# The gate products of a bidirectional RG-LRU as pairs of 64-row tiles, with the gates brought together by transfers on chip

## The chip, the core and the metric

The kernel runs on one core of one Trainium2 chip. The metric is device microseconds (us) of one execution; the number for a kernel is the median of its runs. TensorE (PE) does the matrix products into PSUM banks, ScalarE (ACT) does casts, activations and most evictions of banks, VectorE (DVE) does element-wise work and the recurrence scans, and the DMA queue that SyncE (SP) issues brings the weights in. Each engine works through its own instructions in the order in which they stand in the program and waits in that order.

## What is computed

Two layers of a diffusion backbone over 768 tokens (256 of context, 512 latent) of width 1024. Each layer mixes tokens by four branches (retention, latent attention, RG-LRU, Mamba-2), merges them by gates, and runs a gated feed-forward network. The change touches the RG-LRU alone:

```python
def gates(u, d):
    ub = u.reshape(b, t, LRU_BLOCKS, LRU_BLOCK)          # 8 blocks of 64 channels
    z = jnp.einsum('btnc,gncd->gbtnd', ub, gate_w[d])    # g: two gates, r and i
    z = z.reshape(2, b, t, w) + gate_b[d]
    r, i = jax.nn.sigmoid(z[0]), jax.nn.sigmoid(z[1])
    log_a = -LRU_C * r * jax.nn.softplus(-lam[d])
    return jnp.exp(log_a), jnp.sqrt(-jnp.expm1(2.0 * log_a)) * (i * u)
# run(u, d): a, bb = gates(u, d); h = linear scan h[t] = a[t] * h[t-1] + bb[t]
# both directions d, context first, and the latent tokens from its last state
```

## The kernel before, in words

Channels lie on the 128 partitions and tokens along the free axis. Every product is done as three float32r matmuls (`mm3`, L219 to L222): operands are split into a rounded high part and a low part, and high·high, high·low and low·high are summed in one PSUM bank. A weight of 512 KB is loaded by SP (L198, tile wr), its high part is cast by ACT (L205, tile wh), and its low part is a subtraction on DVE (L143, tile wl).

The 512 channels of the recurrence are four groups f of 128, and each group holds two of the 64-channel blocks. `project(f)` makes the convolved input u and the gelu gate (two products with eight row blocks each; evictions L511 and L1045 on ACT, the convolution on DVE at L152). `scan(f, d)` is called for both directions d, so there are 4 groups x 2 directions x 2 layers = 16 scans. A scan

- splits u (direction 0 alone) by the cast at L216 on ACT and the subtraction at L143 on DVE;
- forms both gates z as products with a 128x128 weight in which the two 64x64 blocks stand on the diagonal and the rest is zero, for a segment of 256 and one of 512 tokens: 4 banks (pool `c`, four banks in all), 12 matmuls;
- evicts each bank by a Tanh on ACT (L1066) into t0 (gate r) or t1 (gate i), 128 partitions each;
- forms the decay on ACT by an Exp (L1069) and a Tanh (L1070) of t0 and a Sqrt (L1074, which has a table load ahead of it), and on DVE the products with t1 and the scan itself (L1079 to L1082).

The bias column of each gate is in the small tile gb, half the stored bias (L549 to L551). The gate weights of two groups come as one 128x1024 load (L1056).

The order of instructions is set ahead of time by a planner that weaves the recurrence into the `merge` of an earlier branch: long runs of PE products (L220 to L222 into banks of pool `g`, also four) are put between the steps of a scan, and the merge's evictions (Tanh, L1334, on ACT) stand among the scan's activations. In layer 0, runs of small products at L317 for the modulation are put in as well (in tiles of 128 rows by 32 columns). The recurrence of layer 0 lies at about 765 to 950 us of the span, that of layer 1 at about 2240 to 2380 us.

Of the kernel before, what the change touches and what calls it, by code (L numbers as in the profile page):

```python
# [8 lines left out]
F32 = mybir.dt.float32  # L9
F32R = mybir.dt.float32r  # L10
AF = mybir.ActivationFunctionType
# [20 lines left out]
SEG_C = (0, CTX)  # L32
# [66 lines left out]
def trunk(tc, xin, cc, const, pv, pr, rows, ada_b, ada_w, w_in, w_uq, w_ukv, w_lg, w_br, w_out, w_up, w_dn, out):  # L99
# [3 lines left out]
    def nm(p):  # L103
        uid[0] += 1
        return f"{p}{uid[0]}"
# [3 lines left out]
    with ExitStack() as ctx:  # L109
# [14 lines left out]
        def S(dt=F32, w=T):  # L124
            return cur[-1].tile([P, w], dt, tag="q" if w == 512 and len(cur) == 2 else "s", name=nm("s"), **({"bufs": N_HALF} if w == 512 and len(cur) == 2 else {}))
# [4 lines left out]
        def C():  # L130
            return pc.tile([P, 512], F32, tag="c", name=nm("c"))
# [13 lines left out]
        def ts(o, a, s1, op0, s2=None, op1=None):  # L145
            if s2 is None:
                dve.tensor_scalar(out=o, in0=a, scalar1=s1, scalar2=None, op0=op0)
            else:
                dve.tensor_scalar(out=o, in0=a, scalar1=s1, scalar2=s2, op0=op0, op1=op1)
# [51 lines left out]
        def unit(ap, f=1024, shape=None):  # L201
            with tc.high_priority(offset=O_UNIT):
                raw = whole(ap, f)
                hi = W4("wh", N_WH)
                act.copy(hi[:, 0:f], raw[:, 0:f])  # L205
                lo = W4("wl", N_WL)
                for c in range(0, f, 512):
                    e = min(f, c + 512)
                    tt(lo[:, c:e], raw[:, c:e], hi[:, c:e].bitcast(F32), SUB)
            if shape is None:  # L210
                return hi, lo
            a, b = shape
            return (hi[:, 0:f].rearrange("p (a b) -> p a b", a=a), lo[:, 0:f].rearrange("p (a b) -> p a b", a=a))

        def split(src, hi, lo):
            act.copy(hi, src)  # L216
            tt(lo, src, hi.bitcast(F32), SUB)
# [302 lines left out]
        def layer_prep(l):  # L520
            q = {}
            v = lp.tile([P, NPV], F32, tag="pv", name=nm("pv"))
            sy.dma_start(out=v, in_=pv[l])
            r = lp.tile([P, NPR], F32, tag="pr", name=nm("pr"))
            sy.dma_start(out=r, in_=pr[l:l + 1, :].to_broadcast([P, NPR]))

            def V(name, a=0, b=None):
                o, w = _PO[name]
                return v[:, o + a:o + (w if b is None else b)]

            q["V"] = V

            z = small(16, "z")
            dve.tensor_copy(z[:, 0:8], r[:, 0:8])
            dve.tensor_copy(z[:, 8:16], V("lam"))
            u = small(16, "z")
            exp_negabs(u, z, 16)
            lgp = small(16, "z")
            log1p_of(lgp, u, 16)
            lg = lp.tile([P, 8], F32, tag="lgr", name=nm("lgr"))  # L540
            stt(lg, z[:, 0:8], 0.0, lgp[:, 0:8], MIN, SUB)
            spv = small(16, "z")
            ts(spv[:, 0:8], z[:, 8:16], -1.0, MUL, 0.0, MAX)
            tt(spv[:, 0:8], spv[:, 0:8], lgp[:, 8:16], ADD)
            l4 = lp.tile([P, 16], F32, tag="l4", name=nm("l4"))
            ts(l4[:, 0:8], spv[:, 0:8], -4.0, MUL)
            ts(l4[:, 8:16], spv[:, 0:8], 4.0, MUL)
            q["l4"] = l4
            gb = lp.tile([P, 16], F32, tag="gb", name=nm("gb"))  # L549
            ts(gb, V("lgb"), 0.5, MUL)  # L550
            q["gb"] = gb  # L551
            q["lg"] = lg

            gn = lp.tile([P, 8], F32, tag="gn", name=nm("gn"))
            o = _PO["gn_w"][0]
            ts(gn, v[:, o:o + 8], 0.5, MUL)
            q["gn"] = gn
            scw = lp.tile([P, 40], F32, tag="scw", name=nm("scw"))
            o = _PO["scw"][0]
            ts(scw, v[:, o:o + 40], 0.5, MUL)  # L560
            q["scw"] = scw
            fcg = lp.tile([P, 88], F32, tag="fcg", name=nm("fcg"))
            ts(fcg[:, 0:66], V("fcw", 0, 66), 0.5, MUL)
            ts(fcg[:, 66:88], V("fcb", 0, 22), 0.5, MUL)
            q["fcg"] = fcg

            q["dtb"] = r[:, 8:24]
            a = lp.tile([P, 1, 16], F32, tag="sa", name=nm("sa"))
            act.activation(out=a[:, 0, :], in_=r[:, 24:40], func=AF.Exp)
            ts(a[:, 0, :], a[:, 0, :], -1.0, MUL)  # L570
            q["a"] = a
            q["dskip"] = r[:, 40:48]
            return q
# [454 lines left out]
        def lru(q, W, WG, hT, full, outs):  # L1028
# [5 lines left out]
            def project(f):  # L1034
# [14 lines left out]
                act.activation(out=t[:, osl], in_=t[:, osl], func=AF.Tanh, scale=GELU_C)  # L1049
                stt(gg[:, osl], t[:, osl], 1.0, gg[:, osl], ADD, MUL)  # L1050

            def scan(f, d):
                u = uu[f]
                if d == 0:
                    if f % 2 == 0:
                        gm[0] = unit(WG(f // 2), shape=(8, 128))  # L1056
                    gm[1] = (S(F32R), S(F32R))
                    split(u, *gm[1])
                t0, t1, a_ = S(), S(), S()
                for g, dst in ((0, t0), (1, t1)):  # L1060
                    i = 4 * (f % 2) + 2 * d + g
                    j = 8 * d + 4 * g + f
                    for off, n in (SEG_C, SEG_L):
                        z = C()
                        mm3(z[:, 0:n], gm[0][0][:, i, :], gm[0][1][:, i, :], gm[1][0][:, off:off + n], gm[1][1][:, off:off + n], True, True)
                        act.activation(out=dst[:, off:off + n], in_=z[:, 0:n], func=AF.Tanh, scale=0.5, bias=q["gb"][:, j:j + 1])  # L1066
                c = 4 * d + f
                nsp, psp = q["l4"][:, c:c + 1], q["l4"][:, 8 + c:9 + c]
                act.activation(out=a_, in_=t0, func=AF.Exp, scale=nsp, bias=nsp)  # L1069
                act.activation(out=t0, in_=t0, func=AF.Tanh, scale=psp, bias=psp)  # L1070
                s = S()
                tt(s, a_, a_, MUL)
                stt(s, s, 1.0, t0, ADD, MUL)
                act.activation(out=s, in_=s, func=AF.Sqrt, scale=0.25)  # L1074
                stt(t1, t1, 1.0, u, ADD, MUL)
                tt(s, s, t1, MUL)
                h_ = S()
                if d == 0:
                    dve.tensor_tensor_scan(out=h_, data0=a_, data1=s, initial=0.0, op0=MUL, op1=ADD)  # L1079
                else:  # L1080
                    dve.tensor_tensor_scan(out=h_[:, 0:CTX][:, ::-1], data0=a_[:, 0:CTX][:, ::-1], data1=s[:, 0:CTX][:, ::-1], initial=0.0, op0=MUL, op1=ADD)
                    dve.tensor_tensor_scan(out=h_[:, CTX:T][:, ::-1], data0=a_[:, CTX:T][:, ::-1], data1=s[:, CTX:T][:, ::-1], initial=h_[:, 0:1], op0=MUL, op1=ADD)  # L1082
                return h_
# [627 lines left out]
```

## Time and profile before

| | |
|---|---|
| median of 3 runs | 2871.04 us (2869.3 to 2872.69) |
| profiled execution | 2870.0 us, of which the span from first to last instruction is 2868.3 us |
| PE busy | 2814.1 us, 98% of the span |
| DVE / ACT busy | 1870.4 us (65%) / 1244.8 us (43%) |
| DMA queue of SP | 38.4% of 16 engines' span |
| mean granted TensorE clock | 0.996 |

"Busy" is the time in which an engine has an instruction under way. Matmuls are pipelined, so the step from one start to the next is what a product costs. In a timeline, "[1.24 <-DVE s L152]" behind an instruction says that its engine sat idle for 1.24 us ahead of it and what ended that; rows with "xN" put N instructions of one kind together.

### The profile page before, as it was taken

What the parts mean: (1) busy time and instruction counts of PE and PEld (TensorE: products, weight loads), DVE (VectorE), ACT (ScalarE), POOL (GpSimd) and SP (SyncE); (2) the same over time, 40 slices, a digit from 0 to 9 for tenths busy, and PEclk for the clock granted to TensorE, in tenths of its full rate; (3) what the DMA queues carried; (4) which work ended last, traced back from release to release, by engine and by line L of the source; (5) the groups of instructions that cost most, each with busy time, mean ns of one, the idle gap of its engine ahead of it and who ended that gap; (6) DMA issues with size and microseconds to landing.
All of it is one profiled execution on the core that took longest, in us unless ns stands there. A gap on an engine that the chain in (4) does not pass through costs nothing.

```text
span 2868.3 us, 41922 instructions
## 1 busy us (share of the span) xinstructions
PE 2814.1 (98%) x16208; PEld 2412.6 (84%) x16208; DVE 1870.4 (65%) x3915; ACT 1244.8 (43%) x2190; POOL 53.3 (2%) x70
## 2 busy tenths in 40 slices
PE   8999999999999999999999999999999999899998
PEld 5999879888988886888888779988888888688887
DVE  6553438767576448855557886545887685886667
ACT  4323325434455325533335653244545573453353
POOL 0000000000000001000000000000000000000000
PEclk9999999999999999999999999999999999999999
DMA  7212441445343345412126563121134334543365
GB/s 260 71 38 94 166 156 38 147 170 186 126 167 117 108 154 190 132 61 67 60 83 199 192 204 112 51 90 60 45 106 141 106 115 141 201 154 96 96 200 175
DMA packets 117974, 363.75 MB, mean 127 GB/s; under 512 B 13920, under 2 KB 14816, under 8 KB 117776
## 3 DMA queue, kind: packets, MB, share of 16 engines
q1 hardware_dynamic: 117776, 361.08, 38.4%
q8 instruction: 127, 2.08, 0.3%
q14 instruction: 71, 0.58, 0.1%
HBM read 332.59 MB, written 26.35 MB: 125 GB/s over the span
## 4 chain that ended last, share of the span: by engine, by line
PE 83%; DVE 8%; DMA 4%; ACT 2%; issue 1%; POOL 1%; SPq 0%; POOLq 0%; DVEq 0%; ACTq 0%
PE g L220 18%; PE g L221 18%; PE g L222 18%; PE g L252 4%; PE g L251 4%; PE g L250 4%; PE g L487 3%; PE g L490 3%; PE g L491 3%; DVE wl L143 2%; DMA wr<-in_w_dn_dram 2%; DVE o L143 1%; PE g L317 1%; DVE st L350 1%; PE c L220 1%
## 5 line engine op out<-in xcount | busy, mean ns | idle before, releaser
L143 DVE TENSOR_TENSOR wl<-wr,wh 128x512 fp32r<-128x512 f32 x866 | 566.7, 681 | 443.8 <-ACT wh L205 438.8
L220 PE MATMUL g<-hh,wh 128*128 128x512 f32 (+1 forms) x2384 | 842.7, 353 | 0.8 <-DVE s L152 0.8
L221 PE MATMUL g<-hl,wh 128*128 128x512 f32 (+1 forms) x2384 | 838.2, 352 | 0.0
L222 PE MATMUL g<-hh,wl 128*128 128x512 f32 (+1 forms) x2384 | 837.4, 351 | 0.0
L205 ACT CAST wh<-wr 128x1024 fp32r<-128x1024 f32 (+1 forms) x433 | 451.6, 1045 | 635.5 <-PE g L221 329.0
L220 PEld LDWEIGHTS g<-hh,wh 128*128 128x128 f32 x2384 | 451.3, 189 | 66.4 <-issue 6.6
L222 PEld LDWEIGHTS g<-hh,wl 128*128 128x128 f32 x2384 | 451.0, 189 | 58.5
L221 PEld LDWEIGHTS g<-hl,wh 128*128 128x128 f32 x2384 | 451.3, 189 | 56.8
L250 PE MATMUL g<-wh,hh 128*128 128x256 f32 (+1 forms) x816 | 232.2, 286 | 0.0
L252 PE MATMUL g<-wl,hh 128*128 128x256 f32 (+1 forms) x816 | 232.0, 285 | 0.0
L251 PE MATMUL g<-wh,hl 128*128 128x256 f32 (+1 forms) x816 | 231.7, 284 | 0.1
L143 DVE TENSOR_TENSOR s<-s,s 128x256 f32<-128x256 f32 (+4 forms) x332 | 206.5, 644 | 36.0 <-ACT s L1074 14.6
L487 PE MATMUL g<-wh,t 128*128 128x512 f32 x468 | 184.0, 395 | 3.0 <-ACT t L216 2.2
L490 PE MATMUL g<-wh,t 128*128 128x512 f32 x468 | 183.1, 393 | 1.4 <-DVE t L143 1.3
L491 PE MATMUL g<-wl,t 128*128 128x512 f32 x468 | 182.2, 392 | 1.0 <-DVE wl L143 0.7
L221 PE MATMUL g<-s,wh 128*128 128x512 f32 (+1 forms) x452 | 160.6, 355 | 0.0
L220 PE MATMUL g<-s,wh 128*128 128x512 f32 (+1 forms) x452 | 160.3, 355 | 0.0
L222 PE MATMUL g<-s,wl 128*128 128x512 f32 (+1 forms) x452 | 159.9, 354 | 0.0
L250 PEld LDWEIGHTS g<-wh,hh 128*128 128x128 f32 x816 | 156.9, 192 | 1.1 <-issue 0.8
L251 PEld LDWEIGHTS g<-wh,hl 128*128 128x128 f32 x816 | 156.9, 192 | 0.8 <-DVE hl L143 0.6
L252 PEld LDWEIGHTS g<-wl,hh 128*128 128x128 f32 x816 | 156.8, 192 | 0.1
L152 DVE SCALAR_TENSOR_TENSOR s<-g,pv,s 128x511 f32<-128x511 f32 (+2 forms) x176 | 111.6, 642 | 61.7 <-ACT s L511 59.8
(289 smaller groups left out, 4136.6 us busy)
## 6 DMA issues: line engine op xcount, KB each, us to landing
wr<-in_w_in_dram SPq DMA_DIRECT2D x144, 512.0 KB, 3.6
wr<-in_w_dn_dram SPq DMA_DIRECT2D x110, 512.0 KB, 4.1
wr<-in_w_up_dram SPq DMA_DIRECT2D x100, 512.0 KB, 3.6
wh<-in_ada_w_dram SPq DMA_DIRECT2D x46, 512.0 KB, 3.7
wl<-in_ada_w_dram SPq DMA_DIRECT2D x46, 512.0 KB, 4.9
wr<-in_w_out_dram SPq DMA_DIRECT2D x40, 512.0 KB, 4.2
wr<-in_w_br_dram SPq DMA_DIRECT2D x32, 512.0 KB, 3.6
acc<-s SPq DMA_DIRECT2D x24, 384.0 KB, 3.4
```

Source lines behind the costliest of these rows:

```text
L143: dve.tensor_tensor(out=o, in0=a, in1=b, op=op)
L152: dve.scalar_tensor_tensor(out=o, in0=a, scalar=s, in1=b, op0=op0, op1=op1)
L205: act.copy(hi[:, 0:f], raw[:, 0:f])
L220: pe.matmul(o, lhsT=sh, rhs=mh, start=start, stop=False)
L221: pe.matmul(o, lhsT=sh, rhs=ml, start=False, stop=False)
L222: pe.matmul(o, lhsT=sl, rhs=mh, start=False, stop=stop)
L250: pe.matmul(o, lhsT=sh, rhs=wkh, start=first, stop=False, skip_group_check=True)
L251: pe.matmul(o, lhsT=sl, rhs=wkh, start=False, stop=False, skip_group_check=True)
L252: pe.matmul(o, lhsT=sh, rhs=wkl, start=False, stop=last, skip_group_check=True)
L487: pe.matmul(ps[a][h], lhsT=xh, rhs=wh[:, cs], start=k == 0, stop=wl is None and k == nk - 1)
L490: pe.matmul(ps[a][h], lhsT=xl, rhs=wh[:, cs], start=False, stop=False)
L491: pe.matmul(ps[a][h], lhsT=xh, rhs=wl[:, cs], start=False, stop=k == nk - 1)
```

## The change

The weights of a scan are now the compact 64-row blocks: rows 0 to 63 of the tile hold both gates of the first block (128 columns), rows 64 to 127 those of the second. A product is a pair of matmuls with 64 rows each, on the upper and the lower half of the array, each into a bank of its own. So a bank holds gate r of one block on partitions 0 to 63 and gate i of the same block on 64 to 127. ACT evicts whole banks as before (four Tanh, now L1087) into two tiles `both[0]` and `both[1]`. Four transfers from SBUF to SBUF, 64x768 elements each and issued by ACT (L1092), then put gate r of both blocks into t0 and gate i into t1. The rest of the scan is the same. gb is gathered by four small transfers of SP for each layer, and the gate weights come as two loads of 64x8x64 elements with one 128x512 cast and one subtraction.

```diff
+            src = pv[l][:, o:o + 16].rearrange("p (d g f) -> p d g f", d=2, g=2)
+            for b in range(2):
+                for g in range(2):
+                    sy.dma_start(out=gb[64 * g:64 * g + 64, 8 * b:8 * b + 8].rearrange("p (d f) -> p d f", d=2), in_=src[64 * b:64 * b + 64, :, g, :])
+            ts(gb, gb, 0.5, MUL)
...
+            def blocks(ap):
+                with tc.high_priority(offset=O_UNIT):
+                    raw, hi, lo = W4("wr", N_WR, F32), W4("wh", N_WH), W4("wl", N_WL)
+                    src = ap.rearrange("p (m b c) -> p m b c", m=8, b=2)
+                    for b in range(2):
+                        r = slice(64 * b, 64 * b + 64)
+                        sy.dma_start(out=raw[r, 0:512].rearrange("p (m c) -> p m c", m=8), in_=src[r, :, b, :])
+                    split(raw[:, 0:512], hi[:, 0:512], lo[:, 0:512])
+                return hi, lo
...
+                i = 4 * (f % 2) + 2 * d
+                both = [S(), S()]
+                for off, n in (SEG_C, SEG_L):
+                    z = [C(), C()]
+                    for p, (w, x) in enumerate(((0, 0), (0, 1), (1, 0))):
+                        for b in range(2):
+                            r = slice(64 * b, 64 * b + 64)
+                            pe.matmul(z[b][:, 0:n], lhsT=gm[0][w][r, 64 * i:64 * i + 128], rhs=gm[1][x][r, off:off + n], start=p == 0, stop=p == 2)
+                    for b in range(2):
+                        j = 8 * b + 4 * d + f
+                        act.activation(out=both[b][:, off:off + n], in_=z[b][:, 0:n], func=AF.Tanh, scale=0.5, bias=q["gb"][:, j:j + 1])
+
                 t0, t1, a_ = S(), S(), S()
                 for g, dst in ((0, t0), (1, t1)):
-                    i = 4 * (f % 2) + 2 * d + g
-                    j = 8 * d + 4 * g + f
-                    for off, n in (SEG_C, SEG_L):
-                        z = C()
-                        mm3(z[:, 0:n], gm[0][0][:, i, :], gm[0][1][:, i, :], gm[1][0][:, off:off + n], gm[1][1][:, off:off + n], True, True)
-                        act.activation(out=dst[:, off:off + n], in_=z[:, 0:n], func=AF.Tanh, scale=0.5, bias=q["gb"][:, j:j + 1])
+                    for b in range(2):
+                        act.dma_start(out=dst[64 * b:64 * b + 64, :], in_=both[b][64 * g:64 * g + 64, :])
```

**ACT, the first scan of layer 1, before.** The four evictions L1066 (s is an SBUF slot, c a bank), then the Exp L1069, with a cast of a weight (L205) ahead of the Tanh L1070, and the merge's eviction L1334 behind the Sqrt:

```order
L1066 ACTIVATE s_21949<-c_21952,gb_14383 128x256
L1066 ACTIVATE s_21949<-c_21957,gb_14383 128x512
L1066 ACTIVATE s_21950<-c_21962,gb_14383 128x256
L1066 ACTIVATE s_21950<-c_21967,gb_14383 128x512
L1069 ACTIVATE s_21951<-s_21949,l_14380 128x768
L205 CAST wh_22201<-wr_22199 128x1024
L1070 ACTIVATE s_21949<-s_21949,l_14380 128x768
L1074 ACT_TABLE_LOAD
L1074 ACTIVATE s_21974<-s_21974 128x768
L1334 ACT_TABLE_LOAD
L1334 ACTIVATE s_22034<-g_21989 128x512
```

The same place after the change (L1087 is L1066 of before, L1095 and L1096 are L1069 and L1070, L1100 is L1074):

```order
L1087 ACTIVATE s_22005<-c_22007,gb_14435 128x256
L1087 ACTIVATE s_22006<-c_22008,gb_14435 128x256
L1087 ACTIVATE s_22005<-c_22017,gb_14435 128x512
L1087 ACTIVATE s_22006<-c_22018,gb_14435 128x512
L1092 DMA s_22027<-s_22005 64x768
L1092 DMA s_22027<-s_22006 64x768
L1092 DMA s_22028<-s_22005 64x768
L1092 DMA s_22028<-s_22006 64x768
L1095 ACTIVATE s_22029<-s_22027,l_14432 128x768
L205 CAST wh_22269<-wr_22267 128x1024
L1096 ACTIVATE s_22027<-s_22027,l_14432 128x768
L1100 ACT_TABLE_LOAD
```

The four transfers stand between the last eviction and the Exp that reads what the first two bring; nothing else of ACT's work stands between them.

**PE, the second scan of layer 0, before.** The scan's products (bank c) and the first product of a run at L317 (bank g); the rest of the scan's products stood behind that run:

```order
L220 MATMUL c_8254<-s_8079,wh_8074 128x256
L221 MATMUL c_8254<-s_8080,wh_8074 128x256
L222 MATMUL c_8254<-s_8079,wl_8076 128x256
L220 MATMUL c_8259<-s_8079,wh_8074 128x512
L221 MATMUL c_8259<-s_8080,wh_8074 128x512
L317 MATMUL g_8241<-wh_8233,silu 32x512
```

After the change, the last eight of the scan's twelve products and the first of the run at L317:

```order
L1084 MATMUL c_8263<-s_8083,wl_8078 128x256
L1084 MATMUL c_8264<-s_8083,wl_8078 128x256
L1084 MATMUL c_8273<-s_8083,wh_8077 128x512
L1084 MATMUL c_8274<-s_8083,wh_8077 128x512
L1084 MATMUL c_8273<-s_8084,wh_8077 128x512
L1084 MATMUL c_8274<-s_8084,wh_8077 128x512
L1084 MATMUL c_8273<-s_8083,wl_8078 128x512
L1084 MATMUL c_8274<-s_8083,wl_8078 128x512
L317 MATMUL g_8251<-wh_8243,silu 32x512
```

The two matmuls of a pair stand side by side and go to two banks, and all twelve now stand ahead of L317. A scan of direction 1 is one such run of twelve; one of direction 0 is a run of four (the high·high pairs) and a run of eight, with a few products of the merge or the projection between them. That makes 24 runs in the program.

**SP, the start of the program, before.** The small parameter tiles pv and pr and then weights:

```order
L523 DMA pv_539<-in_pv_dram 128x277
L525 DMA pr_541<-in_pr_dram 128x48
L198 DMA wr_697<-in_w_in_dram 128x1024
L198 DMA wr_763<-in_w_in_dram 128x1024
L198 DMA wr_829<-in_w_in_dram 128x1024
```

After the change:

```order
L523 DMA pv_539<-in_pv_dram 128x277
L525 DMA pr_541<-in_pr_dram 128x48
L555 DMA gb_579<-in_pv_dram 64x2x4 x4
L198 DMA wr_701<-in_w_in_dram 128x1024
L179 DMA s_596<-in_const_dram 128x768
L198 DMA wr_767<-in_w_in_dram 128x1024
```

The four gathers of gb stand ahead of the weight load wr_701, and one load of constants has moved ahead of the next weight.

## Rows read from the trace of the kernel before

**Rows 1.** The page: busy time by engine, and the chain that ended last.
```profile
PE 2814.1 (98%) x16208; PEld 2412.6 (84%) x16208; DVE 1870.4 (65%) x3915; ACT 1244.8 (43%) x2190; POOL 53.3 (2%) x70
PE 83%; DVE 8%; DMA 4%; ACT 2%; issue 1%; POOL 1%; SPq 0%; POOLq 0%; DVEq 0%; ACTq 0%
```

**Rows 2.** Windows over both recurrences: start:end, length, busy by engine, clock, DMA share, GB/s.
```profile
775.00:905.00 130.00, 129.96 (x771) 108.70 (x770) 91.53 (x123) 79.88 (x104) 0.00 (x0) 1.00 0.42 144
2215.00:2395.00 180.00, 180.00 (x868) 150.94 (x867) 132.67 (x189) 116.03 (x149) 0.00 (x0) 1.00 0.38 123
```

**Rows 3.** Timeline of PE, layer 1, first scan: start, length, engine, line, out<-in.
```profile
2250.42 0.96 PE L220 MATMUL c<-s,wh 128*128 128x256 f32 x4
2251.23 0.40 PE L221 MATMUL g<-hl,wh 128*128 128x512 f32 x1
...
2251.93 0.28 PE L221 MATMUL c<-s,wh 128*128 128x256 f32 x1
...
2253.35 0.40 PE L221 MATMUL g<-hl,wh 128*128 128x512 f32 x1
```

**Rows 4.** Timeline of PE, layer 0: 128x32 tiles at L317 inside a scan's products.
```profile
876.39 0.40 PE L221 MATMUL c<-s,wh 128*128 128x512 f32 x1
876.71 0.62 PE L317 MATMUL g<-wh,silu 128*32 128x512 f32 x1
...
877.17 0.59 PE L317 MATMUL g<-wh,silu 128*32 128x512 f32 x1
...
878.57 0.50 PE L222 MATMUL c<-s,wl 128*128 128x512 f32 x1
878.90 0.28 PE L220 MATMUL c<-s,wh 128*128 128x256 f32 x1
```

**Rows 5.** Timeline of ACT, layer 1, the two scans of the first group.
```profile
2252.38 2.10 ACT L1066 ACTIVATE s<-c,gb 128x256 f32<-128x256 f32 x4 [0.82 <-PE c L222]
2254.36 1.03 ACT L1069 ACTIVATE s<-s,l 128x768 f32<-128x768 f32 x1
...
2260.73 0.60 ACT L1334 ACTIVATE s<-g 128x512 f32<-128x512 f32 x1
2261.22 1.99 ACT L1066 ACTIVATE s<-c,gb 128x256 f32<-128x256 f32 x4
...
2272.67 0.60 ACT L1334 ACTIVATE s<-g 128x512 f32<-128x512 f32 x1
```

**Rows 6.** DMA between SBUF tiles (L616) and to the accumulator (L1345): issue in ns, landing.
```profile
L616 SPq DMA_DIRECT2D s<-s x16: 461/568/602, 65.3 to 1778.8; - x16
DMA to landing us min/median/max: 2.4/3.9/5.5
...
L1345 SPq DMA_DIRECT2D acc<-s x48: 319/327/373, 279.6 to 2381.0; - x48
...
DMA to landing us min/median/max: 2.3/3.4/5.9
```

**Rows 7.** Timelines of PE and ACT, layer 1: PE behind ACT's evictions.
```profile
2276.51 0.39 PE L220 MATMUL g<-hh,wh 128*128 128x512 f32 x1
...
2379.19 0.62 ACT L216 CAST s<-s 128x512 fp32r<-128x512 f32 x1 [1.24 <-DVE s L152]
...
2380.32 0.39 PE L220 MATMUL g<-s,wh 128*128 128x512 f32 x1
```

**Rows 8.** Timelines of ACT and PE, layer 0, first group.
```profile
788.21 0.87 ACT L1334 ACTIVATE s<-g 128x512 f32<-128x512 f32 x2
...
790.72 0.62 PE L317 MATMUL g<-wh,silu 128*32 128x512 f32 x1
...
806.09 0.84 ACT L216 CAST s<-s 128x768 fp32r<-128x768 f32 x1 [5.06 <-DVE s L152]
```

**Rows 9.** Timeline of SP's queue at the start of the program.
```profile
28.87 0.33 SPq L525 DMA_DIRECT2D pr<-in_pr_dram  x1
30.22 0.33 SPq L198 DMA_DIRECT2D wr<-in_w_in_dram  x1
```

More of the change, by code (lines that the diff above doesn't have):

```diff
@@ L549, in layer_prep @@
             gb = lp.tile([P, 16], F32, tag="gb", name=nm("gb"))
-            ts(gb, V("lgb"), 0.5, MUL)
+            o = _PO["lgb"][0]
+            src = pv[l][:, o:o + 16].rearrange("p (d g f) -> p d g f", d=2, g=2)
[3 more added lines that the diff above has]
+            ts(gb, gb, 0.5, MUL)
             q["gb"] = gb
@@ L1055, in scan @@
                     if f % 2 == 0:
-                        gm[0] = unit(WG(f // 2), shape=(8, 128))
+                        gm[0] = blocks(WG(f // 2))
                     gm[1] = (S(F32R), S(F32R))
                     split(u, *gm[1])
+                i = 4 * (f % 2) + 2 * d
[9 more added lines that the diff above has]
+                        act.activation(out=both[b][:, off:off + n], in_=z[b][:, 0:n], func=AF.Tanh, scale=0.5, bias=q["gb"][:, j:j + 1])
                 t0, t1, a_ = S(), S(), S()
                 for g, dst in ((0, t0), (1, t1)):
-                    i = 4 * (f % 2) + 2 * d + g
-                    j = 8 * d + 4 * g + f
-                    for off, n in (SEG_C, SEG_L):
-                        z = C()
-                        mm3(z[:, 0:n], gm[0][0][:, i, :], gm[0][1][:, i, :], gm[1][0][:, off:off + n], gm[1][1][:, off:off + n], True, True)
-                        act.activation(out=dst[:, off:off + n], in_=z[:, 0:n], func=AF.Tanh, scale=0.5, bias=q["gb"][:, j:j + 1])
+                    for b in range(2):
+                        act.dma_start(out=dst[64 * b:64 * b + 64, :], in_=both[b][64 * g:64 * g + 64, :])
                 c = 4 * d + f
```

## The prediction

> **What bounds the kernel now.** I read the page's busy times first and its chain of waits second [rows 1]. PE is busy for 98% of the span, and 83% of the chain that ended last is PE. So a change counts through two things: time taken off PE's own row of products, and time in which PE is made to wait. The windows over the two recurrences [rows 2] say the same for the stretches that the change touches: PE 129.96 of 130 us in layer 0 and 180.00 of 180 in layer 1, at a granted clock of 1.00 (the 2.4 GHz level). There is nothing to win there but PE's products. ACT is busy for 79.88 and 116.03 us in them, so it has some 50 and 64 us idle. The reader should keep that sum apart from the question where the idle time lies, because the forecast turns on it.
>
> **What PE gains.** In the first scan of layer 1 the four high·high products take from 2250.42 to 2251.23 us, and the eight others from 2251.93 to 2253.35 [rows 3]: 0.81 + 1.42 = 2.23 us for a scan, 35.7 us for 16 scans. Twelve instructions stay twelve. If the two of a pair run side by side, half is saved: 17.8 us. Does the trace show tiles side by side? At L317 four tiles of 128x32 run in each round; the first two rounds begin at 876.71 and 877.17, and three rounds take from 877.17 to 878.57 [rows 4]. That is about 0.45 us for four 512-column products, where four in turn at the 0.23 us of a plain product would need 0.92. So tiles do overlap, but these divide the columns of the array, not its rows. The low end is that the two weight loads of a pair go one after another. The mean load is 2412.6/16208 = 0.149 us [rows 1], a pair would then cost 0.30 us, and six pairs 1.8 us against 2.13 (six times the 1.42/4 of one 256- and one 512-column product): 0.33 us for a scan, 5 us in all. I take the side-by-side end, since L317 is the nearest row.
>
> Against it stands the change of tile shape. The step from the last full product into L317 is 0.32 us (876.39 to 876.71) against 0.23 for its kind, and the first step behind the run is 0.33 us (878.57 to 878.90) [rows 4]; with a tenth ahead of 878.57 an excursion costs 0.2 to 0.3 us. There are 24 runs, so 5 to 7 us. PE's own balance is 11 to 13 us saved at best, and 2 us lost at worst.
> The Trainium skill, "TensorEngine Tiling (Array Packing)", Theoretical Speedup, gives up to 2x for a dimension of at most 64, and its Key Properties say that changing the tiling mode drains the engine. The rows at L317 agree with the drain (0.2 to 0.3 us), and no row of this kernel shows row tiles; by the page alone the balance is the better end.
>
> **What ACT is made to wait.** Before, the Exp L1069 starts at 2254.36, while the four evictions that began at 2252.38 are just ending [rows 5]. After, it stands behind four transfers and reads what the first two bring. I call S the time from the last eviction to the Exp. The rows nearest to these transfers are L616 (128 KB, SBUF to SBUF) and L1345 (384 KB) against 192 KB here [rows 6]: an issue takes 0.32 us (L1345) to 0.57 us (L616), and the landing comes at least 2.3 to 2.4 us, in the median 3.4 to 3.9 us, after it. The second transfer is issued one issue later than the first, so S is at least 0.32 + 2.3 = 2.6 us, and by L616's row 0.57 + 2.4 = 3.0 at its fastest and 0.57 + 3.9 = 4.5 at its median. L616 is the nearer kind; I take the middle of its two, 3.7 us. All four issues (1.3 to 2.3 us) fit inside that. What waits behind the Exp on ACT are the weight casts L205, the Tanh, the table load, the Sqrt, and the merge's eviction L1334; PE needs the bank that L1334 empties, and the next group's u.
>
> How much lands on PE follows from what PE has in hand behind these. **Layer 1.** ACT runs without a gap from the first scan's evictions (2252.38) through L1334 at 2260.73 and the second scan's evictions at 2261.22 [rows 5], so the second scan starts S late and L1334 at 2272.67 is late by 2S. It ends at 2273.27, and PE writes its bank next at 2276.51 [rows 5, 7]: 3.2 us in hand. The delay is 2S − 3.2 for each of three groups. Work that PE has saved by then makes no difference: it only arrives earlier at the same wait. Behind the fourth group the merge's product at 2380.32 starts 0.51 us after the cast at 2379.19 has ended [rows 7], so 2S − 0.7 with what little ACT idles ahead of it. Layer 1 comes to 8S − 10.3: at 3.7 us, 19.3 us. **Layer 0.** Here the first scan's stall hits L1334 at 788.21. Its first eviction ends 0.6 us later, and L317 takes the bank at 790.72 [rows 8], 1.9 us in hand; the same pair stands in the next groups with 1.9 to 2.5. The second scan's stall goes mostly into gaps such as the 5.06 us ahead of 806.09, though that gap ends with DVE's part of the scan, which the stall moves too [rows 8]. I take one stall in each of four groups, 4S − 6, with 5S − 8 as the other reading: 8.8 to 10.5 us.
>
> The sum is 12S − 16.3. For S = 3.7 it is +28 us, for 2.6 it is +15, for 3.0 +20, for 4.5 +38. PE's gain is in it already, because PE would spend it waiting; the drains too.
>
> **The smaller parts.** The evictions keep their count and shapes, so nothing changes there. The compact gate weights halve two casts and loads in each layer; ACT has idle time ahead of them, and I put that at nothing (a whole cast of 1 us twice a layer, 4 us, if it were on the path). gb's four gathers stand ahead of a weight load at the start, where SP issues only every 1.35 us (28.87 to 30.22) [rows 9]: that load leaves up to 5.4 us later, and if PE had nothing else by then it would cost all of that; PE has the norm's products there, and I take 0, with 0 to 5 as bounds. Layer 1's gathers and the doubled loads of gate weights lie far ahead of their use.
>
> So the profiled execution of 2870.0 us becomes 2898, and the median, which lies 1.0 us above it, 2899 us.
>
> **Rivals.** *The stalls are absorbed, and PE keeps its gain.* ACT has 114 us idle in the two stretches [rows 2], and 16 stalls of 3.7 us are only 59. If the transfers land in 1.4 us or less (the point where 12S − 16.3 is zero), or the casts that wait for PE in between take up the delay, the 11 us of PE's balance remain: 2860 us. For it speaks the idle sum; against it that no transfer of 128 KB or more landed under 2.3 us [rows 6] and that ACT has no gap where the stall comes [rows 5].
> *The transfers hinder each other.* Four of them are in flight at once beside weight loads that fill 0.38 to 0.42 of the queues' time [rows 2]. If the second transfer moves only when the first has landed, S is 2.4 + 2.4 = 4.8 us, and by L616's maximum 5.5 us: 12S − 16.3 is +41 to +50, so 2912 to 2921 us.
> The Trainium skill, "DMA: Bandwidth & Descriptors", Rules for kernel authors, says that two transfers to disjoint partition halves serialize and should be one, which is this case; no row here shows two halves in flight undisturbed, and the median of 3.9 us against a minimum of 2.4 leaves room for it.
> *The pairs do not run side by side.* PE then has nothing in hand from the change, and the drains come on top where PE isn't waiting: 2 to 7 us more than the forecast, 2901 to 2906 us.
>
> **How the numbers follow.** The forecast (S of 2.6 to 4.5 us) has a chance of 0.61 and gives 2886 to 2909 us; with unoverlapped pairs (0.07) up to 2906. Transfers that hinder each other have 0.17: 2912 to 2921. Absorbed stalls have 0.15, of which 0.10 end faster by over 0.2% (the size that a measurement of this kernel can tell from no change) and 0.05 within it. So faster 0.10, same 0.05, slower 0.85. The range leaves out the faster tenth and a little on either side: 2870 to 2920 us.
>
> **What would show it.** Right: gaps of 3 to 4.5 us on ACT ahead of the Exp, released by a DMA, 16 times; PE waiting in both recurrences for ACT's L1334 (now L1360) or for u's cast; the pairs starting within some 20 ns of each other. Wrong: PE without waits in these windows (then the first rival), gaps near 5 us (the second), or pairs that start 0.1 us and more apart (the third). If the DVE products that read t1, which the last two transfers bring, hold up the low parts of weights, PE would wait for L143 instead, and the delay would be longer than my sum.

## The result, and the profile after

The change takes 2935.99 us (median of 4 runs, 2933.5 to 2939.98) against 2871.86 us for the kernel before: 1.0225 times as long, 95% interval 1.0213 to 1.0238, or 64 us more. The prediction had the sign right and less than half of the size: +28 us were forecast, and the time lies above the range.

The page of after, its busy times and its chain, beside [rows 1]:

```profile
PE 2827.0 (96%) x16208; PEld 2407.5 (82%) x16208; DVE 1866.9 (64%) x3911; ACT 1242.6 (42%) x2190; POOL 53.2 (2%) x70
PE 79%; DVE 9%; DMA 5%; ACT 4%; issue 2%; POOL 1%; SPq 0%; ACTq 0%; POOLq 0%; DVEq 0%
```

PE's share of the chain has fallen from 83 to 79%, and ACT and DMA together have gained 3 points. PE is *longer* busy than before (2827.0 against 2814.1 us), although its gate products have become shorter: a first hint that something else than waiting happened to it. The waits of PE (engine, line, what it waited for: us in total, times, longest us); before the change neither recurrence had any of these four kinds:

```profile
PE g L220 <- ACT s L1360: 33.6, 5, 7.9
PE g L317 <- ACT s L1360: 9.6, 4, 3.8
...
PE g L220 <- ACT s L1051: 4.8, 1, 4.8
...
PE g L220 <- ACT s L216: 2.1, 1, 2.1
```

That is 50 us, 43 of them for ACT's merge eviction (L1360 is L1334 of before). ACT's timeline in layer 1, the two scans of the first group, to be held against [rows 5]:

```profile
2274.04 2.00 ACT L1087 ACTIVATE s<-c,gb 128x256 f32<-128x256 f32 x4 [0.90 <-PE c L1084]
2275.49 2.42 ACTq L1092 DMA_DIRECT2D s<-s  x4
2279.32 1.03 ACT L1095 ACTIVATE s<-s,l 128x768 f32<-128x768 f32 x1 [3.29 <-DMA s<-s]
...
2285.99 1.05 ACT L205 CAST wh<-wr 128x1024 fp32r<-128x1024 f32 x1 [1.42 <-PE g L221]
...
2288.85 1.99 ACT L1087 ACTIVATE s<-c,gb 128x256 f32<-128x256 f32 x4
2290.29 3.55 ACTq L1092 DMA_DIRECT2D s<-s  x4
2295.99 1.03 ACT L1095 ACTIVATE s<-s,l 128x768 f32<-128x768 f32 x1 [5.16 <-DMA s<-s]
...
2303.29 0.60 ACT L1360 ACTIVATE s<-g 128x512 f32<-128x512 f32 x1
```

The Exp (L1095) stands 3.29 us behind the evictions in the first scan and 5.16 us in the second. The four issues begin under the last eviction and take 2.42 and 3.55 us, of which 1.87 and 3.00 us lie behind its end (2276.04 and 2290.84). PE's timeline of the same place:

```profile
2273.18 0.40 PE L220 MATMUL g<-hh,wh 128*128 128x512 f32 x1
2273.51 0.39 PE L1084 MATMUL c<-s,wh 64*128 64x256 f32 x2
2273.73 0.28 PE L1084 MATMUL c<-s,wl 64*128 64x256 f32 x2
2273.85 0.40 PE L1084 MATMUL c<-s,wh 64*128 64x512 f32 x2
2274.08 0.40 PE L1084 MATMUL c<-s,wl 64*128 64x512 f32 x2
2274.41 0.50 PE L221 MATMUL g<-hl,wh 128*128 128x512 f32 x1
...
2297.22 0.39 PE L222 MATMUL g<-hh,wl 128*128 128x512 f32 x1
2303.94 0.80 PE L220 MATMUL g<-hh,wh 128*128 128x512 f32 x1 [6.34 <-ACT s L1360]
2304.53 0.63 PE L221 MATMUL g<-hl,wh 128*128 128x512 f32 x1
2304.96 0.63 PE L222 MATMUL g<-hh,wl 128*128 128x512 f32 x1
...
2309.22 0.45 PE L220 MATMUL g<-hh,wh 128*128 128x512 f32 x1
2309.51 0.39 PE L221 MATMUL g<-hl,wh 128*128 128x512 f32 x1
```

Two things are to be read here. A pair costs what one product cost: 0.12 us from 2273.73 to 2273.85 with 256 columns, 0.23 us from 2273.85 to 2274.08 with 512. And PE stands still for 6.34 us until ACT's eviction has ended, and then its products come 0.43 us apart (2304.53 to 2304.96) instead of 0.23, until 2309.22. The windows over that stretch (start:end, length, busy by engine, granted clock, DMA share, GB/s) say why:

```profile
2300.00:2304.00 4.00, 0.06 (x1) 0.06 (x1) 3.93 (x7) 3.85 (x4) 0.00 (x0) 0.81 0.41 116
2304.00:2308.00 4.00, 4.00 (x10) 3.17 (x11) 3.85 (x6) 1.27 (x3) 0.00 (x0) 0.50 0.56 152
2308.00:2312.00 4.00, 4.00 (x16) 3.26 (x15) 3.82 (x8) 0.48 (x1) 0.00 (x0) 0.83 0.17 66
2312.00:2316.00 4.00, 4.00 (x20) 2.89 (x19) 2.88 (x5) 3.41 (x5) 0.00 (x0) 1.00 0.13 41
```

The granted clock fell to 0.50, the 1.2 GHz level, towards the end of the wait, and was back at 1.00 some 5 us after it; in [rows 2] it stood at 1.00 throughout. This is why the page shows PE as longer busy.

Layer 0 shows a third thing. Before, in the first scan of the second group, ACT had no cast of a weight (L205) ahead of the Sqrt; the cast that waits for PE stood behind the merge's two evictions:

```profile
823.97 0.87 ACT L1334 ACTIVATE s<-g 128x512 f32<-128x512 f32 x2
825.61 1.05 ACT L205 CAST wh<-wr 128x1024 fp32r<-128x1024 f32 x1 [0.77 <-PE g L221]
```

After, two casts stand ahead of the Sqrt, and the second of them waits for PE:

```profile
830.49 1.05 ACT L205 CAST wh<-wr 128x1024 fp32r<-128x1024 f32 x1 [1.94 <-PE g L221]
831.55 1.28 ACT L1100 ACT_TABLE_LOAD   x1
...
835.00 0.87 ACT L1360 ACTIVATE s<-g 128x512 f32<-128x512 f32 x2
```

And PE's timeline there:

```profile
831.42 0.40 PE L1084 MATMUL c<-s,wl 64*128 64x512 f32 x2
835.65 1.06 PE L317 MATMUL g<-wh,silu 128*32 128x512 f32 x1 [3.83 <-ACT s L1360]
```

The cast waited 1.94 us for a product of PE (the last reader of its buffer); behind it on ACT stood a table load, the Sqrt, another table load and the eviction; and PE came to a stop after that very product and its gate products, waiting for that eviction. The wait of 3.83 us is a circle PE, ACT, PE, and the length of the stall plays no part in it. The third group has the same 3.83 us, and has it again in e6 below, where the Exp stands 5.0 us behind the evictions instead of 3.3. The fourth group's 4.78 us, with one more cast ahead of the eviction, is 4.80 us in e6.

### The profile page after: what moved, and what is told of

Read it like the earlier page. It is cut to its first block, busy times and chain, and to the rows that moved or that the text cites. A ratio compares the mean times of both kernels' runs of the same rounds, so it can differ in the third digit from the quotient of the medians.

```text
span 2931.8 us, 42044 instructions
## 1 busy us (share of the span) xinstructions
PE 2827.0 (96%) x16208; PEld 2407.5 (82%) x16208; DVE 1866.9 (64%) x3911; ACT 1242.6 (42%) x2190; POOL 53.2 (2%) x70
## 4 chain that ended last, share of the span: by engine, by line
PE 79%; DVE 9%; DMA 5%; ACT 4%; issue 2%; POOL 1%; SPq 0%; ACTq 0%; POOLq 0%; DVEq 0%
PE g L220 17%; PE g L221 17%; PE g L222 17%; PE g L251 4%; PE g L250 4%; PE g L252 4%; PE g L487 3%; PE g L490 2%; PE g L491 2%; DVE wl L143 2%; DMA wr<-in_w_dn_dram 2%; PE g L317 1%; DVE o L143 1%; DVE st L350 1%; ACT wh L205 1%
## 5 line engine op out<-in xcount | busy, mean ns | idle before, releaser
L220 PE MATMUL g<-hh,wh 128*128 128x512 f32 (+1 forms) x2384 | 851.3, 357 | 39.6 <-ACT s L1360 33.6
L205 ACT CAST wh<-wr 128x1024 fp32r<-128x1024 f32 (+1 forms) x429 | 447.2, 1044 | 619.8 <-PE g L221 313.3
L220 PEld LDWEIGHTS g<-hh,wh 128*128 128x128 f32 x2384 | 454.9, 191 | 116.9 <-ACT s L1360 37.8
```

Of the source, the lines that this page charges most:

```text
L220: pe.matmul(o, lhsT=sh, rhs=mh, start=start, stop=False)
```

## The experiments

Theory A is that of the prediction: ACT stands still ahead of the Exp, and PE runs into its waits; the lower clock behind these waits was joined to it after the result. Rivals were that the products in pairs cost time themselves (B), and that the transfers cost by their load on the queues (C). For every kernel I have added up PE's waits (over 0.15 us, from the timelines) and what the lower clock took while PE was busy (one minus the granted clock times the busy time, in windows of 1 us), over 740 to 1000 us and 2200 to 2450 us. "Against before" is the difference of the medians in the same set of runs.

| kernel | median us | against before | PE's waits | lost by the clock |
|---|---|---|---|---|
| the change | 2936.0 | +64.1 | 49.7 | 19.7 |
| e1, no transfers | 2866.5 | −6.7 | 0.6 | 0.0 |
| e2, transfers alone | 2938.1 | +64.9 | 48.6 | 14.0 |
| e3, issued by SP | 2913.2 | +41.4 | 34.8 | 10.6 |
| e4, both directions first | 2929.2 | +56.0 | 37.8 | 11.9 |
| e5, half evictions | 2903.4 | +30.2 | 23.8 | 11.8 |
| e6, 4.2 us of ACT work | 2927.5 | +55.7 | 42.3 | 17.8 |
| e7, both first, by SP | 2912.4 | +40.6 | 26.5 | 9.4 |
| e9, filled waits | 2935.0 | +63.2 | 39.3 | 12.4 |
| e11, 1.7 us of ACT work | 2892.9 | +18.7 | 17.7 | 10.3 |
| e12, transfers in first scans | 2906.3 | +32.1 | 27.2 | 10.8 |
| e13, transfers in second scans | 2915.3 | +41.1 | 34.5 | 14.2 |
| e14, sorted by DVE | 2883.8 | +9.6 | 13.3 | 3.7 |
| e15, sorted by DVE, earlier | 2876.3 | +3.3 | 8.0 | 0.0 |

For the change, e3, e5, e6 and e11 to e15, waits plus clock minus PE's gain (6.7 us, from e1) give the measured difference to within 3 us: for the change 49.7 + 19.7 − 6.7 = 62.7 against 64.1, for e13 42.0 against 41.1, for e15 1.3 against 3.3. Without the clock the change would come out 21 us short, so the clock is a cost beside the waits. This is an account and not an experiment; PE's own busy time, which has grown by 12.9 us in the change, is near the 13.0 us that 19.7 − 6.7 make.

**e1: the pairs without the transfers.**

```diff
-                t0, t1, a_ = S(), S(), S()
-                for g, dst in ((0, t0), (1, t1)):
-                    for b in range(2):
-                        act.dma_start(...)
+                t0, t1 = both
+                a_ = S()
```

> The changed kernel without its four transfers: t0 and t1 are the two tiles into which the banks were evicted, so the gates of the two blocks are left unsorted; all else is as in the change. Theory A (ACT stands still ahead of the Exp, PE runs into its waits and then works at a lower granted clock): PE keeps its gain and nothing waits, 2857 to 2864 us, and no wait of PE for ACT's L1360 line (here 1358) over 0.3 us. Rival B (the pairs of 64 rows, the changes of tile shape or the new order of instructions cost time themselves): 2871 us or more.

2866.46 us, 0.9976 times the kernel before (0.9967 to 0.9985), and no wait in either recurrence but two of 0.3 us. B falls: the pairs, the changes of tile shape and the compact weights save 6.7 us (4 to 9.5). That is less than expected, and less than the 11 to 13 of the prediction.

**e2: the transfers without the pairs.**

```diff
-                t0, t1, a_ = S(), S(), S()
-                for g, dst in ((0, t0), (1, t1)):
+                both = [S(), S()]
+                for g, dst in ((0, both[0]), (1, both[1])):
...
+                t0, t1, a_ = S(), S(), S()
+                for g, dst in ((0, t0), (1, t1)):
+                    for b in range(2):
+                        act.dma_start(out=dst[64 * b:64 * b + 64, :], in_=both[g][64 * b:64 * b + 64, :])
```

> The kernel before with its own products and weights, plus the four transfers alone: t0 and t1 go through four 64x768 transfers issued by ACT, to the same partitions. Theory A, with PE's gain spent in its waits: as slow as the change, 2932 to 2940 us, since PE only arrives later at the same waits. Theory A with a gain that adds up: 2945 to 2950 us. Rival B: 2871 us to 2885 us.

2938.13 us, as slow as the change. Taking PE's gain away changed next to nothing, since PE only came later to the same waits. So the transfers and what follows from them are the loss.

**e6 and e11: ACT held up without any transfer.** The lines against e1:

```diff
                 t0, t1 = both
                 a_ = S()
+                for _ in range(5):      # e11: range(2)
+                    act.copy(a_, t0)
```

> The changed kernel without its four transfers (the gates stay unsorted, as in e1), but with five copies of 128x768 on ACT in each scan, whose results are thrown away: ACT is held for about 4 us a scan, near the change's mean of 4.1 us, and nothing goes over the queues. Theory A (the stall of ACT and what PE's clock then loses is the whole loss): 2925 to 2940 us. Rival C (the transfers' own load on queues and memory makes a good part): 2890 to 2910 us.

> As e6 (no transfers, gates unsorted, useless copies on ACT), with two copies a scan instead of five: ACT is held 1.7 us instead of 4.2. Theory A with the spare time read from the kernel before (1.4 us of stall in every scan costs nothing): 2866 to 2876 us, PE waits of 5 us in all. If every us of stall costs the same (61 us for 4.2): 2890 us.

e6 gives 2927.47 us, inside the band for A: 4.2 us of ACT's time in each scan reproduce 56 of the 64 us with nothing on the queues, and C falls as the main cause. e11 missed. With 1.7 us the loss is still 19 us (25 against e1), where the spare time read from the kernel before should have hidden nearly all of it. Its waits in layer 1 are 2.82, 2.82, 2.82, 2.94 and 2.13 us. Waits of exactly 2.82 us are in e3, e5, e7, e12 and e13 too, whose stalls differ, so they can't be stalls.

**e12 and e13: the transfers in one direction alone.**

```diff
+                if d == 0:              # e13: d == 1
                     t0, t1, a_ = S(), S(), S()
                     ...
+                else:
+                    t0, t1 = both
+                    a_ = S()
```

> The change with its transfers in the scans of direction 0 alone; those of direction 1 take their gates unsorted. The first scans' stall was 3.3 us. Theory A with spare time counted once for a group: nearly all hides in layer 1 (3.2 us in hand), 1.4 to 2 us a group land in layer 0: 2872 to 2880 us. If the loss were shared by stall length (27 of 66 us): 2895 us.

> The change with its transfers in the scans of direction 1 alone; those of direction 0 take their gates unsorted. The second scans' stall was 5.2 to 6.7 us in layer 1. Theory A: 2 to 3 us a group land in layer 1 and about as much in layer 0, with some fall of the clock: 2880 to 2895 us; e12 and this together lose clearly less than the change's 70 us against e1. If the loss were shared by stall length: 2908 us. Rival C (second scans are slow because the transfers of the first load the queues): the stall of the second scans falls to 3.3 us.

2906.26 and 2915.30 us, 32 and 41 us over the kernel before; both missed upwards, and against e1 they sum to 87 us where the change loses 71. In e12 the second scans have no stall at all, the first ones 3.3 us, and yet PE waits in every group of layer 1. ACT's timeline in the first group of e12 (L1364 is the merge's eviction):

```profile
2295.24 1.04 ACT L205 CAST wh<-wr 128x1024 fp32r<-128x1024 f32 x1 [1.37 <-PE g L221]
2296.30 1.28 ACT L1364 ACT_TABLE_LOAD   x1
2297.60 0.60 ACT L1364 ACTIVATE s<-g 128x512 f32<-128x512 f32 x1
```

PE's timeline at the same place:

```profile
2295.04 0.39 PE L222 MATMUL g<-hh,wl 128*128 128x512 f32 x1
2298.25 0.50 PE L220 MATMUL g<-hh,wh 128*128 128x512 f32 x1 [2.82 <-ACT s L1364]
```

This is the circle of layer 0 again: in the planner's new order a cast stands ahead of the eviction that before stood behind it. The cast waits for PE's last products, the table load and the eviction (1.28 + 0.60 us) wait for the cast, and PE waits 2.82 us for the eviction. In order of ACT's program, with c for a weight cast, E, T, Q for Exp, Tanh and Sqrt, M for the merge's eviction and v for the scan's evictions, transfers left out, the first group of layer 1 reads `vvvvEcTQMvvvvEcTcQM` before, and `vvvvEcTQcMvvvvEcTQcM` in e12: four casts ahead of the second eviction instead of three. No run kept the order of before and put the stall into it, so what the new order costs by itself is read from the traces alone. In e13 the second scans' stall in layer 1 is 3.5, 3.6, 3.5 and 6.3 us against 5.2 to 6.7 in the change, but in layer 0 it is 5.7, 7.0, 9.3 and 3.3 us against 5.7, 4.0, 3.3 and 3.3. So the transfers of the first scans are not what makes the second ones slow. The weight loads of SP are what goes with it: in the change, e2, e9 and e13 every stall of over 5 us, 19 in all, has a weight load issued by SP between 0.5 us before and 1 us after ACT's first issue, and none of the shorter ones has. The three of 3.5 to 3.6 us in e13 have an accumulator transfer there and no weight load.

**e3: issued by SP.** One word: `sy.dma_start` for `act.dma_start`.

> The change with its four transfers issued by SP instead of ACT; the planner then puts a cast of a weight (two in the second scans) between the evictions and the Exp. In the change the four issues alone held ACT for 2.4 us or more. Theory A with the landing as the stall: the Exp still waits for the second transfer, about 3 us, of which a cast of 1 us is useful work; 2905 to 2920 us. Theory A with the issues as the stall: the wait falls to under 2 us, 2885 to 2900 us. Rival C (load on the queues, SP's weight loads held up behind the transfers): 2930 us or more, with PE waiting for low parts of weights.

2913.23 us, in the band in which the landing is the stall. The Exp still comes 3.2 to 5.7 us behind the evictions, of which up to two casts are work. What it gave back over the change, 23 us, is shorter waits in layer 1 (17.6 against 31.0 us) and less loss of clock.

**e4 and e7: both directions' products and evictions ahead of either Exp,** the transfers issued by ACT (e4) or SP (e7).

```diff
+                return t0, t1, a_
+
+            def finish(f, d, t0, t1, a_):
+                u = uu[f]
...
+                ready = [scan(f, d) for d in range(2)]
                 for d in range(2):
-                    hh.append(scan(f, d))
+                    hh.append(finish(f, d, *ready[d]))
```

> The change with the products, evictions and transfers of both directions ahead of either Exp: the evictions of direction 1 (2 us) stand between the transfers of direction 0 and the Exp that reads them, and the transfers of direction 1 have the whole first scan to land. Theory A: the stall ahead of the first Exp falls from 3.3 us to about 1.3, the second goes to nothing; 2860 to 2872 us. Rival C (the transfers cost by their load on the queues, wherever the wait stands): 2915 us or more.

> As e4 (both directions' products and evictions ahead of either Exp), with the transfers issued by SP, so that the eight issues of a group (0.58 us each) no longer stand on ACT. Theory A: with issues and most of the landing off ACT's path, the first Exp waits for 1 us or less and the second for nothing: 2866 to 2885 us. What is left above 2866 is the place of the merge's eviction, which now stands behind both directions' evictions. Rival C: 2915 us or more.

2929.21 and 2912.44 us: they missed by 57 and 27 us, and e4 fell into the band that was given to C. The timeline of ACT in e4, layer 1:

```profile
2287.04 3.35 ACTq L1092 DMA_DIRECT2D s<-s  x4
2290.44 2.00 ACT L1087 ACTIVATE s<-c,gb 128x256 f32<-128x256 f32 x4 [2.85 <-PE g L221]
2291.89 2.43 ACTq L1092 DMA_DIRECT2D s<-s  x4
2294.42 1.03 ACT L1099 ACTIVATE s<-s,l 128x768 f32<-128x768 f32 x1 [1.99 <-issue]
```

The Exp no longer waits for a landing, but the issues themselves hold ACT: 2.85 us ahead of the second evictions and 1.99 ahead of the Exp ("issue" names no other releaser). The row names PE as what ended the first of these waits, but by PE's timeline the products into the first banks of the second direction were done by 2287.1, and the four issues end at 2290.39 (2287.04 + 3.35), right ahead of the evictions at 2290.44: it is they that held ACT. So e4 doesn't speak for C, which e6 had left with little, but for a cost of the issues. I had counted the landing as the cost and the issues as hidden in it. In e7 they are gone, and the second evictions and the merge's evictions are still late; besides, the 24 products of both directions need eight banks and the pool has four. The last twelve of them in e7:

```profile
2277.64 0.86 PE L1084 MATMUL c<-s,wh 64*128 64x256 f32 x4
2278.23 0.39 PE L1084 MATMUL c<-s,wl 64*128 64x256 f32 x2
2278.59 1.08 PE L1084 MATMUL c<-s,wh 64*128 64x512 f32 x3
...
2279.74 0.39 PE L1084 MATMUL c<-s,wl 64*128 64x512 f32 x1
2280.07 0.50 PE L221 MATMUL g<-hl,wh 128*128 128x512 f32 x1
```

They take 2.43 us (2277.64 to 2280.07), where a run of twelve in the change takes 1.24 (2279.18 to 2280.42 us). I take the difference for PE waiting bank by bank in steps that the trace counts as busy. From start to next start, the products of all scans at L1084 come to 31.4 us in e4 and in e7 and to 21.9 us in the change (waits left out), which is 9.5 of the 13 and 11 us by which the table's sum misses e4 and e7; but no run took the bank limit away.

**e5: halves evicted straight to their places by ACT,** `both[g][64 * b:64 * b + 64, off:off + n]` from `z[b][64 * g:64 * g + 64, 0:n]`, with no transfers.

> The change without transfers and with the right gates: ACT evicts each half of a bank straight to its place, 8 evictions of 64 partitions for each scan instead of 4 of 128. Theory A: ACT is longer by the four evictions, 2.0 us a scan, which is a stall of S = 2.0 us: 12 x 2.0 - 16.3 = +8 us on the kernel before, 2865 to 2882 us, with PE waits under 2 us and hardly a fall of the granted clock. If a 64-row eviction is shorter than one of 128 rows: 2860 us.

2903.36 us, above the band. An eviction of 64 partitions is as long as one of 128 (0.58 us in the median against 0.59). In e5's timeline the eight take 4.76 us, against 2.10 for four in [rows 5]:

```profile
2263.38 4.76 ACT L1089 ACTIVATE s<-c,gb 64x256 f32<-64x256 f32 x8 [0.89 <-PE c L1084]
```

So ACT was held 2.7 us a scan instead of the 2.0 expected. Three of the four groups of layer 1 again show a wait of 2.82 us, the circle of e12, and the clock took 11.8 us.

**e9: the waits filled with useless products,** 24 of them ahead of the gelu gate's products in the second to fourth group of layer 1.

> The change with 24 useless 512-column products (5.4 us) on PE just ahead of the product that waits for ACT's eviction, in the second to fourth group of layer 1, where PE stood still for 6.3 to 7.9 us in the change. They fill the wait and write a bank that nobody reads. Theory A with the clock as a cost of its own (after each such wait the granted clock stood at 0.5 for some 4 us): PE never stops for long, and the three groups give back 2 to 2.5 us each: 2927 to 2931 us. Without a cost of the clock: the same as the change, 2934 to 2938 us. If the products come late themselves: 2940 us or more.

2934.98 us: not told apart from the change. The three waits fell from 6.3, 7.9 and 7.4 to 1.9, 3.2 and 1.7 us, and the loss by the clock in layer 1 from 10.5 to 4.9 us. But in this run the stalls ahead of the Exp were 3.2 us longer in layer 1, the last group's wait grew from 7.3 to 9.1 us, and 16 us of products were added. It doesn't settle what the clock costs by itself; for that the table's sum stands.

**e14 and e15: the gates sorted by DVE,** which copies gate r across partitions and shifts gate i in an addition; e15 copies by token segment and shifts gate i later. The lines of e15:

```diff
-                        act.dma_start(out=dst[64 * b:64 * b + 64, :], in_=both[b][64 * g:64 * g + 64, :])
+                        dve.tensor_copy(t0[64 * b:64 * b + 64, off:off + n], both[b][0:64, off:off + n])
...
-                stt(t1, t1, 1.0, u, ADD, MUL)
+                for b in range(2):
+                    ts(t1[64 * b:64 * b + 64, :], both[b][64:128, :], 1.0, ADD)
+                tt(t1, t1, u, MUL)
```

> The change with DVE instead of transfers: two copies of 64x768 across partitions make t0, two additions of 1 make t1 (which the product with u needed anyway), and the planner puts a weight cast of 1 us on ACT between the evictions and the Exp. Theory A: the Exp waits for 0.3 to 1 us, less than is free, and PE keeps the gain of e1: 2864 to 2872 us, at or under the kernel before. If DVE's 1.5 to 2 us more a scan hold up the low parts of weights or the scans: 2880 us or more, with PE waiting for DVE L143.

> As e14, with the copies of gate r split by token segment, so that those of the first 256 tokens run under the evictions of the other 512, and with the additions for gate i put behind the Sqrt. In e14 the Exp still came 1.2 to 4 us behind the evictions: the copies took about 1.2 us, and in the second scans one or two casts of weights that stood ahead of the Exp waited for PE. If the stall by the copies counts: 2870 to 2878 us. If the casts that the planner has moved ahead of the Exp count (they still stand there in seven of eight second scans): 2878 to 2884 us, with PE waiting for ACT's merge eviction in steps of the same length in several groups. At best e1's 2866 us.

e14 takes 2883.80 us (1.0033, 1.0020 to 1.0046), e15 2876.32 us (1.0010, 1.0001 to 1.0019). e15 is the full computation without transfers and within 0.2% of the kernel before, but it doesn't beat it, and no version with all gates in place did. In all eight of its first scans the Exp stands 0.5 to 0.8 us behind the evictions, and no clock is lost; in the second scans 2.3 to 3.1 us are left in layer 1, in part casts ahead of the Exp, in part copies that come late. From e15's second group, ACT:

```profile
2299.32 1.07 ACT L205 CAST wh<-wr 128x1024 fp32r<-128x1024 f32 x1
2301.79 1.03 ACT L1094 ACTIVATE s<-s,l 128x768 f32<-128x768 f32 x1 [1.40 <-DVE s L1089]
```

Shortening the stall took away nearly all of the loss, and with it the fall of the clock.

## Why the prediction was right in sign and wrong in size

Three terms of the sum failed, S, 4S − 6 and the clock, which had no term at all; a fourth, the delay in layer 1, came out in part by luck.

**PE's gain.** Right in mechanism: the two of a pair start within 10 ns of each other and take 0.12 and 0.23 us, and it is 0.33 us from the last full product into a run and again from the first full product behind it to the next (2273.18 to 2273.51, 2274.41 to 2274.74), as at L317 [rows 4]. Oversized: 6.7 us measured against 11 to 13. Inside a run the first pair takes 0.22 us (2273.51 to 2273.73) where the next of its kind takes 0.12, and the last one 0.33 us (2274.08 to 2274.41) where 0.23 is its kind. Those four tenths make 0.4 us for an excursion, where 0.2 to 0.3 was taken, or some 10 us for 24 runs: 17.8 − 10 leaves 8 us, inside e1's 4 to 9.5. That the gain is spent in PE's waits was right: e2 has no such gain and ends where the change ends.

**S.** The mean of the 16 stalls is 4.1 us (66.1 us in all), 3.7 was taken. The first scans have 3.2 to 3.8 us, the second ones 3.3 to 6.7. Eleven stalls lie at 3.2 to 4.0 us, in the range read from L616 and around the 3.7; it is five long ones, 5.2 to 6.7 us, that lift the mean. In all five SP issued a weight load of 512 KB and an accumulator transfer of 384 KB within about 2 us of ACT's first issue (at 2290.08 and 2291.37 beside the issues from 2290.29, for one), and by the stalls of e13 it is the weight load that goes with them; but no run took that load away by itself. The issues (2.42 us and more) were said to fit inside the landing; that held for S and was wrong for ACT, as e4 shows.

**Layer 1: 2S − 3.2 a group, 2S − 0.7 for the last.** The sum came out, in part by luck. The prediction said that ACT has no gap where the stall comes, but it had read this as far as the second scan's evictions [rows 5], and behind them two casts waited for PE:

```profile
2265.42 1.05 ACT L205 CAST wh<-wr 128x1024 fp32r<-128x1024 f32 x1 [1.30 <-PE g L221]
...
2268.14 1.05 ACT L205 CAST wh<-wr 128x1024 fp32r<-128x1024 f32 x1 [0.73 <-PE g L221]
```

The four groups had 2.0, 1.1, 2.0 and 1.1 us of such idle time, which could have taken up that much of 2S. It didn't, because in the new order ACT waits for PE at other casts (1.42 us at 2285.99) and one more cast stands ahead of the second eviction of each group (in the second group one of u): that eviction came 9.0, 10.5, 10.0 and 9.1 us later, counted from the group's first gate eviction, which is 2S and half a us. With the stalls measured (8.4, 9.9, 9.5 and 8.5 us a group) the terms give 5.2, 6.7, 6.3 and 7.8, or 26 us. Measured are 31.0 us of waits less half of PE's gain, 27.7 us. The forecast of 19.3 was low by S.

**Layer 0: 4S − 6.** Wrong. Measured are 18.7 us of waits less 3.3, so 15.4 against 8.8 forecast. In the first group both stalls landed (1.41 and 4.84 us), which was the other reading, 5S − 8, in that group. In the second and third the waits are the circle through a moved cast, 3.83 us, where S − 1.9 would be 1.4; the fourth has 4.78 us. The cast's move stands in the order of ACT's instructions, and the prediction gave it no price: it named the casts among what "waits behind the Exp on ACT" and didn't ask which of them waits for PE.

**The clock.** Missing: the sum counts a wait of PE by its length alone and puts the products behind it at full speed. Each of the change's eight waits of 3.8 us and more brought the granted clock to half, until 3.4 to 6.8 us after PE had resumed, and that took 19.7 us in all; with the wait of 1.41 us in layer 0 it did not fall. The kernel before has no such wait in either recurrence, so its rows there could not show the price; the row of its first 40 us, where the clock was granted at 0.83, could have warned (windows of the kernel before, columns as above):

```profile
0.00:40.00 40.00, 26.85 (x137) 16.95 (x138) 24.13 (x71) 10.87 (x23) 3.55 (x10) 0.83 0.89 339
```

So +28 becomes 27.7 + 15.4 + 19.7 = 63 us, against 64 measured: 8 from longer stalls in layer 1, 7 from layer 0, and 20 from the clock make up the miss. The rival in which the pairs do not run side by side fell with the starts of the pairs and with e1. The one in which the stalls are absorbed fell with e2, e6 and the waits. The one in which transfers hinder each other (S of 4.8 to 5.5 us) fell as it was put: four in flight without a weight load beside their first issue give 3.2 to 4.0 us. Stalls as long as it foretold came only beside a weight load, of which it had also spoken.

## What to carry to other kernels

Spare time read between two instructions holds only for the order in which they stand: where a planner fills a new stall with other work, look in its new order for an instruction that waits for the busy engine and now stands ahead of one that this engine waits for, and price that circle by itself. Price a wait of a nearly full TensorE twice, for its length and for the products at the lower granted clock behind it. A transfer on chip that an in-order engine both issues and waits for costs that engine the issues (0.6 us each here) even when the landing is hidden, so four of them, 2.4 us or more, must be weighed against what they save, here 0.4 us of products a scan.

## What the runs showed of the hardware

- A pair of 64-row float32r products on both halves of the array, into two banks, takes the time of one: 0.12 us for 256 columns and 0.23 us for 512. Going from full products to such a run and back cost 0.4 us in four steps of a tenth.
- ACT evicts 64 partitions in no less time than 128: eight evictions in 4.76 us against four in 2.0 to 2.1 us.
- With four 64x768 transfers between SBUF tiles in flight, the Exp that reads the first two started 5.2 to 6.7 us behind the last eviction where SP issued a weight load between 0.5 us before and 1 us after the first issue, and 3.2 to 4.0 us where it did not.
- An issue of a 64x768 transfer held ACT for 0.58 us in the median, and up to 2.25 us. The line's rows of after (instruction: duration in ns, min/median/max):

```profile
L1092 ACTq DMA_DIRECT2D s<-s x64: 468/578/2252, 779.7 to 2423.8; - x64
```

- ACT and DVE can write to other partitions than they read (0 to 63 against 64 to 127): e5 and e15 sort the gates that way, DVE in 0.42 us for 64x512.
- The granted clock fell to 0.50 with each wait of PE of 3.8 us and more in all these runs, and rose again 3.4 to 6.8 us after PE had resumed in the change. For shorter waits the length does not tell: one of 1.68 us in e14 and one of 1.95 us in e11 brought the fall, one of 3.54 us in e3 did not, and of those of 2.82 us some did and some did not.
